# Halved weight loads and equal priority for both parts of h in the first stage of a hybrid decoder layer

## The chip, the core and the metric

The kernel runs on one core of a Trainium2 chip. The metric is the device time of one execution in microseconds; the time before is the median of three runs. The core has a matrix engine (TensorE, PE in the profile, with its weight loads as PEld), a vector engine (VectorE, DVE), an activation engine (ScalarE, ACT), a general engine (GpSimd, POOL), and SyncE (SP), whose queue issues nearly all DMAs here.

## The reference

One decoder layer on a sequence of 256 tokens with 2048 channels, all in float32. Cut to what matters:

```python
h = rms_norm(x, norm_w)                      # 256 x 2048
proj = h @ w_in                              # 2048 x 17440, split into the inputs of three branches
gates = sigmoid(g_logit + b_gate)            # one gate for each branch
y_a = pool_mixer(...)  @ w_br_pool           # causal pooling branch
y_b = ssd_mixer(...)   @ w_br_ssm            # chunked scan branch, gated with silu(z)
y_c = short_conv_mixer(...) @ w_br_conv      # gated short convolution branch
x = x + (gates[0]*y_a + gates[1]*y_b + gates[2]*y_c) @ w_out
return rms_norm(x, final_norm_w)
```

## The kernel before

Every float32 product is made of three matmuls on rounded parts: a number is split into a high part (rounded to the format fp32r) and the rest, and hi*hi, lo*hi and hi*lo are added up in PSUM. For weights `load_split` does this: SyncE loads a block into a buffer `raw` (line 122), ScalarE writes the high part `wh` (line 132), VectorE writes the rest `wl` (line 133). Lines 132 and 133 stand under `tc.high_priority(4000)`: the planner that puts the instructions of each engine in order takes them ahead of instructions that stand up to 4000 places earlier. `raw` has four buffers, `wh` and `wl` have three each. A buffer can be loaded again when all its readers are done.

The stage that the change touches is the first, "z01". It computes the first 832 columns of the projection (32 for dt, 800 for z) as two halves of 416 columns, before the RMS norm of x is known: it multiplies x times the norm's weight, and the norm's factor is applied afterwards. It walks over the 16 row tiles k of the projection (128 input channels each). For each k:

- `load_x` (line 216) loads two tiles of the transposed x at a time, for even k from 2 on.
- `make_h` (lines 201 to 212) makes the two parts of h: the high part on ScalarE (line 205; for k = 0 on VectorE, line 203), the rest on VectorE (line 206). It then squares x on ScalarE for the norm (line 208 for k = 0, line 211 for the others), and GpSimd adds the square to a sum (line 212). Nothing in `make_h` has a raised priority.
- `load_split` loads 128 x 832 weights (416 KB) with one DMA and splits them with one instruction on each of the two engines.
- twelve matmuls of 416 columns follow: for each half and each of the two token tiles hi*wh, lo*wh and hi*wl (lines 141, 142 and 143).

Tiles 0 and 1 of x and the first weights come in two special loads, r0 and r1, which are two of the four `raw` buffers. r0 holds the norm's weights, x of tile 0 and the left half of the weights of tile 0. r1 holds the right half of these weights and x of tile 1. So both are free only when the squares of tiles 0 and 1 have read them too. Below, w1, w2 and so on are the weight loads of tile 1, 2 and so on in the kernel before; the splits of tile 0 are already in halves.

Of the kernel before, what the change touches and what calls it, by code (L numbers as in the profile page):

```python
# [15 lines left out]
P = 128  # L16
D = 2048
SEQ = 256
KT = D // P
# [14 lines left out]
    + [("gate", 4 * b + n, [(O_GATE + 2048 * b + 512 * n, 512)]) for b in (2, 1) for n in range(4)]  # L34
)
XREST = 2
OUT_CHUNKS = (512, 512, 512, 256, 256)


# [24 lines left out]
def chunk_layout(k, widths):  # L64

    res, off = [], 0
    for n in widths:
        k0, ps = 0, []
        for kts in pieces(n, k):
            ps.append((off, k0, kts))  # L70
            off += P * kts * n
            k0 += kts
        res.append((n, ps))
    return res
# [9 lines left out]
def body(ctx, tc, x, xT, first, w_in, w_bp, w_bs, w_bc, w_o, pool_w, rows, smalls, consts, out):  # L84
# [16 lines left out]
    def s2t(name, bufs=2, dt=F32):  # L101
        return s2.tile([P, 512], dt, name=name, tag=name, bufs=bufs)

    def s1t(name, bufs=2):
        return s2.tile([P, SEQ], F32, name=name, tag=name, bufs=bufs)
# [9 lines left out]
    def rawt():  # L115
        return wp.tile([P, 1024], F32, name="raw", tag="raw", bufs=4)

    def load_split(src, off, kts, n, keep=False, raw=None):
        m = kts * n
        if raw is None:  # L120
            raw = rawt()
            dma(out=raw[:, :m], in_=src[off:off + P * m].rearrange("(p m) -> p m", p=P))
        pool, th, tl = (g4, "g4", "g4") if keep else (wp, "wh", "wl")
        wh = pool.tile([P, 1024], F32R, name="wh", tag=th)
        wl = pool.tile([P, 1024], F32R, name="wl", tag=tl)
        if n == 416:

            r, h, l = (w[:, :kts * q].rearrange("p (k n) -> p k n", k=kts)[:, :, :n] for w, q in ((raw, n), (wh, 512), (wl, 512)))
        else:
            r, h, l = (w[:, :m] for w in (raw, wh, wl))  # L130
        with tc.high_priority(4000):
            A.activation(h, r, AF.Copy)  # L132
            V.tensor_tensor(out=l, in0=r, in1=h.bitcast(F32), op=ALU.subtract)  # L133
        return [h, l] if n == 416 else [w.rearrange("p (k n) -> p k n", k=kts) for w in (h, l)]
# [4 lines left out]
    def mm3(acc, hi, lo, wh, wl, n, first, last):  # L139

        T.matmul(acc[:, :n], hi, wh, start=first, stop=False)  # L141
        T.matmul(acc[:, :n], lo, wh, start=False, stop=False)  # L142
        T.matmul(acc[:, :n], hi, wl, start=False, stop=last)  # L143
# [48 lines left out]
    xw = one.tile([P, KT * SEQ + 128], F32, name="xw", tag="yA")  # L192
# [4 lines left out]
    def xk(k):  # L197
        return xw[:, KT + k * SEQ:KT + (k + 1) * SEQ]

    def make_h(k, xr, nw, hi_on_v=False):  # L200
        h = h0[k // 2][:, k % 2]
        if hi_on_v:
            V.tensor_scalar(h[:, 0], xr, nw, None, op0=ALU.mult)
        else:
            A.activation(h[:, 0], xr, AF.Copy, scale=nw)  # L205
        V.scalar_tensor_tensor(out=h[:, 1], in0=xr, scalar=nw, in1=h[:, 0].bitcast(F32), op0=ALU.mult, op1=ALU.subtract)  # L206
        if k == 0:
            A.activation(sqs, xr, AF.Square)
        else:
            sq = s1t("cin")  # L210
            A.activation(sq, xr, AF.Square)
            G.tensor_tensor(out=sqs, in0=sqs, in1=sq, op=ALU.add)

    def load_x(k0, kts):
        a, b = KT + k0 * SEQ, KT + (k0 + kts) * SEQ
        dma(out=xw[:, a:b], in_=xT[:, a:b])
# [4 lines left out]
    def h0parts(k):  # L221
        return h0[k // 2][:, k % 2, 0], h0[k // 2][:, k % 2, 1]
# [10 lines left out]
    r0, r1 = rawt(), rawt()  # L233
# [3 lines left out]
    G.tensor_copy(xw[:, :KT], r0[:, :KT])  # L237
    for off, k, _ in where["z01", 0][1]:
        if k == 0:
            make_h(0, r0[:, KT:KT + SEQ], r0[:, :1], True)  # L240
            ws = [load_split(None, 0, 1, 416, raw=r) for r in (r0[:, KT + SEQ:], r1)]
            ws = [(wh[:, 0], wl[:, 0]) for wh, wl in ws]
        else:
            if k >= XREST and k % 2 == 0:
                load_x(k, 2)
            make_h(k, r1[:, 416:416 + SEQ] if k == 1 else xk(k), xw[:, k:k + 1])
            wh, wl = load_split(w_in, off, 2, 416)
            ws = [(wh[:, i], wl[:, i]) for i in range(2)]
        hi, lo = h0parts(k)
        for acc, (wh, wl) in zip(zacc, ws):  # L250
            for t in range(2):
                ts = slice(t * P, (t + 1) * P)
                mm3(acc[t], hi[:, ts], lo[:, ts], wh, wl, 416, k == 0, k == KT - 1)
    load_x(0, XREST)
    sm = one.tile([P, S_END], F32, name="sm")
# [236 lines left out]
    for g, w in enumerate(WIN):  # L492
# [6 lines left out]
        s, back, i = u0, 1, 1  # L499
        while back < w:  # L500
            nxt = win[i]
            V.tensor_tensor(out=nxt[:, :, PAD:], in0=s[:, :, PAD:], in1=s[:, :, PAD - back:PAD + SEQ - back], op=ALU.add)
            s, back, i = nxt, 2 * back, 3 - i
# [15 lines left out]
    for g in range(4):  # L519
        acc = in_channels("pg", g)  # L520
        yq = channels(pool_w, [(g * P * 512, 0, 2)], dhl[g], 2, [pss.tile([P, 512], F32, name="yq", tag="ss") for _ in range(2)])
        for b in range(2):
            k = 2 * g + b
# [34 lines left out]
    for j in range(4):  # L558
# [4 lines left out]
        for b, acc in enumerate(in_channels("cc", j)):  # L563
# [3 lines left out]
            k = 2 * j + b  # L567
# [40 lines left out]

    nch = len(OUT_CHUNKS)
    sso = one.tile([P, 2, nch], F32, name="sso")  # L610
# [32 lines left out]
    c0 = 0  # L643
    for i, (n, ps) in enumerate(chunk_layout(KT, OUT_CHUNKS)):
        fr = s2t("nw", bufs=2)
# [8 lines left out]
        else:  # L654
# [5 lines left out]
            ws = [load_split(w_o, off, kts, n, True) for off, _, kts in ps]  # L660
            for t in range(2):
                ts = slice(t * P, (t + 1) * P)
                for (wh, wl), (_, k0, kts) in zip(ws, ps):
                    for j in range(kts):
                        k = k0 + j
# [89 lines left out]
```

## Time and profile before

| | before |
|---|---|
| median of 3 runs | 1071.35 us (1070.44 to 1071.42) |
| profiled execution | 1071.29 us |
| its span, first to last instruction | 1069.2 us |
| PE busy | 1059.0 us (99%) |
| DVE busy | 715.5 us (67%) |
| ACT busy | 541.5 us (51%) |
| read from HBM | 208.57 MB, 197 GB/s over the span |

The profile is of one execution, whose span is 2.09 us shorter than its time. PE is busy nearly all the time, so the few places where it waits are what there is to look at; the views of these places are printed below, ahead of the prediction. Times in a row are microseconds from the start of the span unless marked ns.

### The profile page before, as it was taken

How to read it: one execution, taken by the hardware profiler on the slowest of the kernel's cores; microseconds unless marked ns; L12 is line 12 of the kernel's file. 1: busy time of each engine (PE TensorE's matmuls, PEld its weight loads, DVE VectorE, ACT ScalarE, POOL GpSimd, SP SyncE). 2: the span in 40 equal slices, each digit the busy share in tenths (PEclk: the TensorE clock that was granted, in tenths of full speed). 3: DMA queues.
4: the chain of work that ended last, by engine and by line, in shares of the span. 5: the costliest groups of instructions: out<-in, count | busy, mean ns of one | idle time of the engine just before them, and what ended most of it. 6: DMA issues, size and time to landing. Idle time of an engine off the chain costs nothing.

```text
span 1069.2 us, 14489 instructions
## 1 busy us (share of the span) xinstructions
PE 1059.0 (99%) x5486; PEld 917.1 (86%) x5486; DVE 715.5 (67%) x1011; ACT 541.5 (51%) x723; POOL 22.2 (2%) x35
## 2 busy tenths in 40 slices
PE   8999999999999999999999999999999999999997
PEld 7999888888888888888888888888888888888887
DVE  7596878777777666776875967565555555555564
ACT  7575666564465444554654645443444444444452
POOL 4100000000000000000000000000000000000000
PEclk9999999999999999999999999999999999999999
DMA  8766555555556566665556554555656666555663
GB/s 282 242 191 221 203 196 179 187 176 189 178 177 213 195 210 206 197 206 182 193 192 197 187 193 175 182 206 200 198 201 202 205 205 205 203 193 181 233 212 125
DMA packets 63141, 211.65 MB, mean 198 GB/s; under 512 B 6944, under 2 KB 7904, under 8 KB 63072
## 3 DMA queue, kind: packets, MB, share of 16 engines
q1 hardware_dynamic: 62784, 210.21, 58.6%
q8 instruction: 43, 0.70, 0.3%
q10 hardware_dynamic: 288, 0.52, 0.1%
q14 instruction: 26, 0.21, 0.1%
HBM read 208.57 MB, written 2.13 MB: 197 GB/s over the span
## 4 chain that ended last, share of the span: by engine, by line
PE 98%; issue 1%; DMA 0%; DVE 0%; ACT 0%; SPq 0%; POOLq 0%; POOL 0%; DVEq 0%
PE acc L169 25%; PE acc L142 19%; PE acc L143 19%; PE acc L141 19%; PE acc L173 13%; PE yp L457 1%; PE tp L410 1%; DMA raw<-w_in_c 0%; PE yq L169 0%; PE yo L463 0%; PE tpx L396 0%; PE yq L173 0%; PE cb L430 0%; DVE h L206 0%; ACT wh L132 0%
## 5 line engine op out<-in xcount | busy, mean ns | idle before, releaser
L133 DVE TENSOR_TENSOR wl<-raw,wh 128x1024 fp32r<-128x1024 f32 (+3 forms) x381 | 455.4, 1197 | 276.6 <-ACT wh L132 273.1
L132 ACT ACTIVATE wh<-raw 128x1024 fp32r<-128x1024 f32 (+3 forms) x381 | 394.3, 1036 | 382.8 <-PE acc L142 280.5
L169 PE MATMUL acc<-hl,wh 128*128 128x512 f32 x1152 | 280.0, 393 | 0.0
L169 PEld LDWEIGHTS acc<-hl,wh 128*128 128x128 f32 x1152 | 210.9, 188 | 41.4 <-issue 1.2
L173 PEld LDWEIGHTS acc<-hl,wl 128*128 128x128 f32 x1152 | 147.8, 191 | 5.6
L173 PE MATMUL acc<-hl,wl 128*128 128x256 f32 x1152 | 149.9, 283 | 0.0
L143 PE MATMUL acc<-wl,hl 128*128 128x512 f32 x384 | 149.4, 389 | 0.0
L142 PE MATMUL acc<-wh,hl 128*128 128x512 f32 x384 | 149.4, 389 | 0.0
L141 PE MATMUL acc<-wh,hl 128*128 128x512 f32 x384 | 149.4, 389 | 0.0
L142 PEld LDWEIGHTS acc<-wh,hl 128*128 128x128 f32 x384 | 72.1, 188 | 15.1
L141 PEld LDWEIGHTS acc<-wh,hl 128*128 128x128 f32 x384 | 72.1, 188 | 15.0
L143 PEld LDWEIGHTS acc<-wl,hl 128*128 128x128 f32 x384 | 72.1, 188 | 14.8
L185 ACT COPY half<-acc 128x256 f32<-128x256 f32 x72 | 26.3, 367 | 78.5 <-PE acc L169 78.5
L141 PE MATMUL acc<-wh,h 128*128 128x416 f32 x160 | 56.0, 353 | 1.2 <-ACT h L205 1.2
L142 PE MATMUL acc<-wh,h 128*128 128x416 f32 x160 | 56.3, 352 | 0.5 <-DVE h L206 0.5
L143 PE MATMUL acc<-wl,h 128*128 128x416 f32 x160 | 56.0, 351 | 0.0
L141 PE MATMUL acc<-wh,mT 128*128 128x512 f32 (+1 forms) x160 | 55.5, 348 | 0.0
L142 PE MATMUL acc<-wh,mT 128*128 128x512 f32 (+1 forms) x160 | 55.5, 347 | 0.0
L143 PE MATMUL acc<-wl,mT 128*128 128x512 f32 (+1 forms) x160 | 55.3, 347 | 0.0
L141 PE MATMUL acc<-wh,yh 128*128 128x512 f32 x128 | 50.0, 390 | 0.0
L143 PE MATMUL acc<-wl,yh 128*128 128x512 f32 x128 | 49.8, 389 | 0.0
L142 PE MATMUL acc<-wh,yl 128*128 128x512 f32 x128 | 49.8, 389 | 0.0
(183 smaller groups left out, 1035.0 us busy)
## 6 DMA issues: line engine op xcount, KB each, us to landing
raw<-w_in_c SPq DMA_DIRECT2D x240, 512.0 KB, 3.5
raw<-w_bs_c SPq DMA_DIRECT2D x32, 512.0 KB, 3.9
raw<-w_o_c SPq DMA_DIRECT2D x32, 512.0 KB, 4.1
raw<-w_in_c SPq DMA_DIRECT2D x39, 416.0 KB, 3.8
raw<-w_bp_c SPq DMA_DIRECT2D x16, 512.0 KB, 3.7
raw<-w_bc_c SPq DMA_DIRECT2D x16, 512.0 KB, 3.3
nw<-rows SPq DMA_DIRECT2D x19, 256.0 KB, 4.2
gm<-cumd SPq DMA_DIRECT2D x8, 512.0 KB, 5.0
```

The lines of the kernel that those rows point to most:

```text
L132: A.activation(h, r, AF.Copy)
L133: V.tensor_tensor(out=l, in0=r, in1=h.bitcast(F32), op=ALU.subtract)
L141: T.matmul(acc[:, :n], hi, wh, start=first, stop=False)
L142: T.matmul(acc[:, :n], lo, wh, start=False, stop=False)
L143: T.matmul(acc[:, :n], hi, wl, start=False, stop=last)
L169: T.matmul(acc[b], wh[:, j, b * P:(b + 1) * P], hl[:, k].rearrange("p i s -> p (i s)"), start=k == 0, stop=k == kt - 1)
L173: T.matmul(acc[b][:, SEQ:], wl[:, j, b * P:(b + 1) * P], hl[:, k, 0], start=False, stop=False)
L185: A.copy(half, acc[:, SEQ:])
L410: T.transpose(out=tp[:, b], in_=src[:, b * P:(b + 1) * P], identity=ident)
L457: T.matmul(yp[:, 64 * h:64 * h + 64], gm[:, h], xd[:, 64 * h:64 * h + 64], start=True, stop=True)
```

## The change

The weights of row tiles 1 to 3 are loaded in two DMAs of 208 KB (128 x 416) in place of one of 416 KB, and split by two instructions on each engine in place of one; the array in HBM is laid out to suit (for tile 0 the halves came in r0 and r1 already). Both parts of h are made under the same raised priority as the splits of weights. The squares leave `make_h`, keep their ordinary priority and now stand behind the load and the split of the tile's weights.

```diff
+HALVES = 4
...
         V.scalar_tensor_tensor(out=h[:, 1], in0=xr, scalar=nw, in1=h[:, 0].bitcast(F32), op0=ALU.mult, op1=ALU.subtract)
+
+    def square(k, xr):
         if k == 0:
             A.activation(sqs, xr, AF.Square)
...
     for off, k, _ in where["z01", 0][1]:
         if k == 0:
-            make_h(0, r0[:, KT:KT + SEQ], r0[:, :1], True)
+            with tc.high_priority(4000):
+                make_h(0, r0[:, KT:KT + SEQ], r0[:, :1], True)
             ws = [load_split(None, 0, 1, 416, raw=r) for r in (r0[:, KT + SEQ:], r1)]
             ws = [(wh[:, 0], wl[:, 0]) for wh, wl in ws]
         else:
             if k >= XREST and k % 2 == 0:
                 load_x(k, 2)
-            make_h(k, r1[:, 416:416 + SEQ] if k == 1 else xk(k), xw[:, k:k + 1])
-            wh, wl = load_split(w_in, off, 2, 416)
-            ws = [(wh[:, i], wl[:, i]) for i in range(2)]
+            with tc.high_priority(4000):
+                make_h(k, r1[:, 416:416 + SEQ] if k == 1 else xk(k), xw[:, k:k + 1])
+            if k < HALVES:
+                ws = [load_split(w_in, off + P * 416 * i, 1, 416) for i in range(2)]
+                ws = [(wh[:, 0], wl[:, 0]) for wh, wl in ws]
+            else:
+                wh, wl = load_split(w_in, off, 2, 416)
+                ws = [(wh[:, i], wl[:, i]) for i in range(2)]
+        square(k, r0[:, KT:KT + SEQ] if k == 0 else r1[:, 416:416 + SEQ] if k == 1 else xk(k))
...
         if s == "z01":
-            flat[:P * n * KT] = w.reshape(-1)
+            flat[:P * n * HALVES] = w[:HALVES].reshape(HALVES, P, 2, 416).transpose(0, 2, 1, 3).reshape(-1)
+            flat[P * n * HALVES:P * n * KT] = w[HALVES:].reshape(-1)
```

## Rows read from the trace of the kernel before

**Rows 1.** The page, part 4: chain that ended last, shares of the span by engine.

```profile
PE 98%; issue 1%; DMA 0%; DVE 0%; ACT 0%; SPq 0%; POOLq 0%; POOL 0%; DVEq 0%
```

**Rows 2.** Waits of PE, whole span: who waited for whom: total, times, longest.

```profile
PE acc L141 <- ACT h L205: 1.2, 1, 1.2
...
PE acc L142 <- DVE h L206: 0.5, 1, 0.5
```

**Rows 3.** Busy by stretch: from:to, length, engines' busy (instructions), granted clock, DMA, GB/s.

```profile
7.00:8.20 1.20, 0.08 (x1) 0.08 (x1) 0.50 (x1) 1.20 (x3) 0.00 (x0) 1.00 1.00 373
...
9.66:1052.00 1042.34, 1042.30 (x5386) 903.51 (x5387) 706.72 (x991) 533.71 (x711) 19.60 (x23) 1.00 0.59 199
```

**Rows 4.** Timeline, weight loads of PE: start, length, instruction, [idle before, releaser].

```profile
6.41 0.19 PEld L143 LDWEIGHTS acc<-wl,h 128*128 128x128 f32 x1
8.12 0.68 PEld L141 LDWEIGHTS acc<-wh,h 128*128 128x128 f32 x4 [1.52 <-ACT h L205]
9.66 0.19 PEld L142 LDWEIGHTS acc<-wh,h 128*128 128x128 f32 x1 [0.86 <-DVE h L206]
...
11.09 0.19 PEld L141 LDWEIGHTS acc<-wh,h 128*128 128x128 f32 x1
...
15.61 0.19 PEld L141 LDWEIGHTS acc<-wh,h 128*128 128x128 f32 x1
```

**Rows 5.** Timeline of ACT, from the second split to h of tile 1.

```profile
4.48 0.55 ACT L132 ACTIVATE wh<-raw 128x416 fp32r<-128x416 f32 x1 [0.28 <-DMA raw<-first]
4.94 0.40 ACT L208 ACTIVATE xc<-raw 128x256 f32<-128x256 f32 x1
6.77 0.90 ACT L132 ACTIVATE wh<-raw 128x832 fp32r<-128x832 f32 x1 [1.43 <-DMA raw<-w_in_c]
7.58 0.49 ACT L205 ACTIVATE h<-raw,xw 128x256 fp32r<-128x256 f32 x1
```

**Rows 6.** Timeline of DVE, from the splits of tile 0 to h of tile 1.

```profile
4.46 1.19 DVE L133 TENSOR_TENSOR wl<-raw,wh 128x416 fp32r<-128x416 f32 x2
7.70 1.02 DVE L133 TENSOR_TENSOR wl<-raw,wh 128x832 fp32r<-128x832 f32 x1 [2.05 <-ACT wh L132]
8.64 0.96 DVE L206 SCALAR_TENSOR_TENSOR h<-raw,xw,h 128x256 fp32r<-128x256 f32 x1
```

**Rows 7.** Timeline of SP's queue: issue of w1, w4, x of tiles 14 and 15, w13 and w14.

```profile
1.65 0.42 SPq L122 DMA_DIRECT2D raw<-w_in_c  x1
...
8.76 0.33 SPq L122 DMA_DIRECT2D raw<-w_in_c  x1
...
23.75 0.42 SPq L216 DMA_DIRECT2D xw<-x_chn  x1
26.07 1.26 SPq L122 DMA_DIRECT2D raw<-w_in_c  x2
```

**Rows 8.** Waits of SP's queue, first 12 us.

```profile
SPq L122 <- ACT xc L208: 0.3, 1, 0.3
```

**Rows 9.** Issue to landing: r0 and r1; w1; w4; x of tiles 2 and 3.

```profile
DMA to landing us min/median/max: 2.9/3.1/3.3
...
DMA to landing us min/median/max: 5.1/5.1/5.1
...
DMA to landing us min/median/max: 3.8/3.8/3.8
...
DMA to landing us min/median/max: 5.6/5.6/5.6
```

**Rows 10.** Groups by line and shape, first 40 us: count, busy us, mean ns, idle before.

```profile
L132 ACT ACTIVATE wh<-raw 128x832 fp32r<-128x832 f32 x16 | 14.2, 895 | 5.9 <-PE acc L142 4.1 <-DMA raw<-w_in_c 1.7
...
L133 DVE TENSOR_TENSOR wl<-raw,wh 128x416 fp32r<-128x416 f32 x2 | 1.2, 588 | 0.0
L132 ACT ACTIVATE wh<-raw 128x416 fp32r<-128x416 f32 x2 | 1.1, 551 | 1.9 <-DMA raw<-first 1.9
L206 DVE SCALAR_TENSOR_TENSOR h<-raw,h 128x256 fp32r<-128x256 f32 x1 | 0.5, 486 | 0.0
```

## The prediction, as it was put on record before the changed kernel ran

> **What bounds the kernel now.** The chain that ended last is PE for 98% [rows 1], so only what moves PE counts. The waits of PE are read next: over the whole span there are two on data, 1.2 us for the high part of h (ScalarE, line 205) and 0.5 us for its rest (VectorE, line 206) [rows 2]. The busy time by stretch confirms it from the other side: from 9.66 to 1052 us PE is busy 1042.30 of 1042.34 us [rows 3]. So all that the change can win lies before 9.66 us, in row tile 1, and what it wins reaches the end unless PE starts to wait somewhere else.
>
> How much is there? The timeline of PE's weight loads has the first load of tiles 2 and 4 at 11.09 and 15.61 [rows 4], so a tile takes PE 2.26 us, and tile 3 starts at 13.35. Tile 0 sends its last load at 6.41, so tile 1 could begin at 6.60 and tile 2 at 6.60 + 2.26 = 8.86. The most that can be won is 11.09 - 8.86 = 2.23 us, 0.21% of the time. The two idle stretches of the loads, 1.52 and 0.86 us [rows 4], are about this sum. 0.2% (2.14 us) is about what a measurement of this kernel can tell from no change.
>
> **Tile 1: h and halves.** ScalarE takes the second split of tile 0 (4.48 to 5.03), the square of tile 0 (to 5.34), then idles 1.43 us until w1 has landed, and makes h of tile 1 only after w1's split, at 7.58 [rows 5]. VectorE idles 2.05 us and makes the rest of h after the split of w1, at 8.64 [rows 6]. With raised priority the high part goes right behind the second split, 5.03 to 5.52 (0.49 [rows 5]); the rest goes behind VectorE's two half splits, which end at 5.65 [rows 6], and takes 0.49 [rows 10], to 6.14. Both are then done before PE wants them at 6.60. The weights: r1 landed at 4.48 [rows 5], and w1, issued at 1.65, 5.1 us later, at 6.75 [rows 7, 9]. The first half, 1a, is half of the bytes between, so about 5.6; the second, 1b, 6.75. A half split takes ScalarE 0.55 and VectorE 0.59 [rows 10]: 1a is split at 6.15 and 6.75, 1b at 7.3 and 7.9. PE wants 1a at 6.60 and 1b 1.13 later, at 7.73, and its first loads are those of the high parts. So tile 1 runs nearly without a wait, and 2.0 to 2.2 us are won at this point. This part I hold for safe.
>
> **What the halves add.** Per tile ScalarE gets 2 x 0.551 - 0.895 = 0.21 us more [rows 10], VectorE 2 x 0.588 - 1.02 = 0.16 [rows 6, 10], for three tiles 0.6 and 0.5. The idle 1.43 and 2.05 us of [rows 5, 6] hide them; without that cover each is paid once. SP gets three more issues of 0.33 to 0.42 us [rows 7], and x of tiles 2 and 3, issued right behind w1 and landed 5.6 us later [rows 9], at 7.7, comes one issue later, at 8.1 at worst. Its h is then made by 9.1, which is where tile 2 is wanted at best. The bytes stay the same. GpSimd's sums are not waited for by PE in this stage.
>
> **Tiles 2 to 4: the buffers.** Here the gain can go. There are four `raw` buffers and three of `wh`, and a half takes a whole one. Before, r0, r1, w1 and w2 filled the four; now r0, r1, 1a and 1b do, so nothing of tile 2 is on its way until a buffer is free. Which one is taken is seen on SP: w4 was issued at 8.76, when VectorE's split of w1 was done (7.70 + 1.02) [rows 6, 7], so the buffer that the planner sees free first is reused; w3 waited for the square of tile 0 [rows 8]. The first half of tile 2 (2a) thus goes out when the square of tile 0 has read r0 or when 1a is split on VectorE, at 6.75 plus the queue's step, 6.9. Were the square put right behind h of tile 1 it would be 5.9.
>
> No row has a half's flight alone. r0 (344 KB, an empty queue) took 2.9 [rows 9]; with 136 KB less at 373 GB/s [rows 3] that is 2.5, the lower bound. w4 (416 KB, shared queue) took 3.8 [rows 9]; with 208 KB less it is 3.2, the upper. I take 2.8. Then 2a lands at 9.7 and is split at 10.25 (ScalarE) and 10.85 (VectorE). Tile 2 begins at 10.25, not at 8.86: of the 2.2 us won 0.8 are left. The load of tile 4, whole again, is the ninth block, so it takes 2a's buffer at best (if every earlier one is free in its turn): issued 10.9, landed 3.8 later at 14.7, split on ScalarE 0.9 later at 15.6. PE began tile 4 at 15.61 before. Nothing is left in the middle of the bounds; with r0's buffer free a little earlier (a flight of 3.3, as r1 [rows 9]) it is 0.5. I take 0.3. Best ends: 2a issued 5.9, flight 2.5, w4's flight 3.3: split at 13.75, gain 1.9. Worst ends: 6.9, 3.2, and w4 4.4 (3.8 and the 0.6 of half a load ahead of it): 16.55, a loss of 0.9. That the low parts of w4 come 1.02 us behind [rows 6] costs nothing if PE is given the high parts of both halves first, as in [rows 4], where four loads of line 141 lead; else up to 0.7. From tile 5 on both the buffers and the loads are as before, and later weights stay ahead of PE [rows 3].
>
> The Trainium skill ("DMA: Bandwidth & Descriptors", Anatomy of one DMA) fits a DMA by about 2.0 us fixed plus its bytes at 436 GB/s, on another issue path than this one: a half gets barely cheaper than a whole. By it, as an estimate, a half flies 2.5 us and a whole 3.0, and tile 4 would be split 1.1 us sooner than in my sum. The trace agrees on the large fixed part for r0, and not on w4, which took 0.8 more [rows 9]; that is why I take the row.
>
> **The rivals.** *All of it is won.* 2a must land by 8.3, so be issued by 5.8 with a flight of 2.5; and w4 must be split by 13.4. Only the earliest place of the square and the lowest bounds come near: 1071.29 - 2.23 = 1069.05. Against it: four buffers.
>
> *Late squares starve the loads.* r0 and r1 come free only with the squares of tiles 0 and 1, and now all splits and all h go ahead of these on ScalarE. And h does not run dry: SP's queue lets x pass blocked weights (x of tiles 14 and 15 went out at 23.75, ahead of w13 and w14 at 26.07 [rows 7]), so h of later tiles is there to push the squares back. Behind ScalarE's queue then stand SP's loads for r0 and r1, and PE behind these. If the square of tile 0 comes only after the split of 3a, two buffers carry all: 2a split on VectorE at 10.85, 3a issued 10.9, landed 13.7, split 14.25: 0.9 later than tile 3 began before. The square then frees r0 at 14.65 (0.40 [rows 5]), w4 lands at 18.45, is split at 19.35, 3.7 us later than before: 1075.0. With the lower flights it is 2.5 us: 1073.8. It decides from where the square of tile 0 starts after 10.9; a square that only comes at 9 to 10 costs nothing. For it: the priorities; against it: ScalarE waits for data between 5 and 8 us [rows 5], where a square fits if the planner sees the gap.
>
> *The halves do nothing.* If 1a lands with 1b, or the planner's order stays, tile 1 is as before but for the extra work: 1071.3.
>
> A longer gap could cost PE its clock; through the 1.5 us gap of before the granted clock stayed at 1.00 [rows 3], so I leave that out.
>
> **How the numbers follow.** Forecast (the buffers eat nearly all): 1071.29 - 0.3 = 1071.0, its own range 1069.4 to 1072.2, chance 0.58. All won, 1069.05: 0.07. Starved by late squares, 1073.8 to 1075.0: 0.23. Nothing, 1071.3: 0.12. The median of the runs stands 0.06 above the profiled execution, which changes nothing. The range to hold 8 in 10 leaves out half of the first rival below and the dearer half of the second above: 1069.2 to 1074.4. Faster by over 0.2% (under 1069.2) is the first rival: 0.07. Slower (over 1073.5) is the second but for its cheapest cases: 0.21. The rest, 0.72, is within.
>
> **What would show it.** Step 1 is right if PE's waits on lines 205 and 206 are gone and tile 1's loads follow 6.60 with under 0.3 us idle. Step 2 is right if PE's new wait is on `wh` of the first half of tile 2 or on tile 4's, with SP waiting for `wl`. The starved case shows as a start of line 208 after 10 us and a wait of over 2 us on `wh` of tile 4. I would be wrong if tile 2 starts before 9.3 us, or if PE waits after tile 5.

## The result, and the profile after

| | before | after |
|---|---|---|
| median (6 runs each) | 1071.38 us (1070.44 to 1072.78) | 1077.1 us (1076.25 to 1077.44) |
| profiled execution | 1071.29 us | 1076.94 us |
| its span | 1069.2 us | 1074.8 us |

After over before is 1.0053, with a 95% interval of 1.0043 to 1.0063: the change costs 0.5%, some 5.7 us, and lies outside the predicted range. The two spans differ by 5.6 us, and that is what the traces have to account for. In the changed file the lines moved: the issue of a weight load is 123, the splits are 133 and 134, the matmuls 142 to 144, h is 206 and 207, and the squares are 211 (tile 0) and 214, with GpSimd's sum in 215.

The first view is again the timeline of PE's weight loads: start, length, instruction, and in brackets the idle time before it with its releaser. The lines are the first load of tiles 1 to 4, and between them the last two loads of tile 1 and one load from the middle of tile 3. They answer [rows 4].

```profile
7.39 0.19 PEld L142 LDWEIGHTS acc<-wh,h 128*128 128x128 f32 x1
...
9.27 0.19 PEld L143 LDWEIGHTS acc<-wh,h 128*128 128x128 f32 x1
9.46 0.19 PEld L144 LDWEIGHTS acc<-wl,h 128*128 128x128 f32 x1
11.62 0.19 PEld L142 LDWEIGHTS acc<-wh,h 128*128 128x128 f32 x1 [1.97 <-ACT wh L133]
...
16.36 0.29 PEld L142 LDWEIGHTS acc<-wh,h 128*128 128x128 f32 x1 [2.56 <-ACT wh L133]
...
18.26 0.33 PEld L142 LDWEIGHTS acc<-wh,h 128*128 128x128 f32 x1
...
21.21 0.19 PEld L142 LDWEIGHTS acc<-wh,h 128*128 128x128 f32 x1 [1.14 <-ACT wh L133]
```

Tile 1 runs without a wait. The waits that stood ahead of it and in its middle have gone to the tiles behind it: 1.97 us before tile 2, 2.56 before tile 3, 1.14 before tile 4, each for the high part of the weights. Twelve loads make a tile, so the same view dates every tile:

| first weight load of | before | after | later by |
|---|---|---|---|
| tile 1 | 8.12 | 7.39 | -0.73 |
| tile 2 | 11.09 | 11.62 | 0.53 |
| tile 3 | 13.35 | 16.36 | 3.01 |
| tile 4 | 15.61 | 21.21 | 5.60 |
| tile 9 | 26.91 | 32.61 | 5.70 |

The whole loss has been made by the start of tile 4. Of the step from tile 3 to tile 4 (4.85 us in place of 2.26), 1.14 us is the wait; the rest is tile 3 itself, whose loads take 0.33 us each and not 0.19. The busy time by stretch shows why: from:to, length, then busy time with instructions of PE, PEld, DVE, ACT and POOL, the granted clock, the DMA share and GB/s. The stretches are tile 2, the gap before tile 3, and most of tile 3.

```profile
11.60:13.80 2.20, 2.18 (x12) 2.17 (x12) 2.20 (x7) 2.20 (x6) 0.00 (x0) 1.00 0.85 289
13.80:16.30 2.50, 0.35 (x2) 0.00 (x1) 0.87 (x3) 2.09 (x8) 1.45 (x2) 1.00 0.85 248
16.36:19.60 3.24, 3.24 (x9) 3.14 (x10) 2.17 (x2) 1.95 (x5) 2.92 (x4) 0.50 0.90 309
```

After the gap the granted clock is 0.50, the lower of the two levels (1.2 GHz). Tile 3 takes 16.36 to 20.07, which is 3.71 us where a tile takes 2.26: 1.45 us of the loss.

Who was late? The next view is ScalarE's timeline, which answers [rows 5].

```profile
4.53 0.55 ACT L133 ACTIVATE wh<-raw 128x416 fp32r<-128x416 f32 x1 [0.42 <-DMA raw<-first]
4.99 0.49 ACT L206 ACTIVATE h<-raw,xw 128x256 fp32r<-128x256 f32 x1
5.62 1.21 ACT L133 ACTIVATE wh<-raw 128x416 fp32r<-128x416 f32 x2
7.42 3.71 ACT L206 ACTIVATE h<-xw 128x256 fp32r<-128x256 f32 x9 [0.58 <-DMA xw<-x_chn]
11.03 0.98 ACT L133 ACTIVATE wh<-raw 128x416 fp32r<-128x416 f32 x2
11.91 2.10 ACT L206 ACTIVATE h<-xw 128x256 fp32r<-128x256 f32 x5
13.91 0.40 ACT L211 ACTIVATE xc<-raw 128x256 f32<-128x256 f32 x1
14.22 0.40 ACT L214 ACTIVATE cin<-raw 128x256 f32<-128x256 f32 x1
...
15.46 0.42 ACT L214 ACTIVATE cin<-xw 128x256 f32<-128x256 f32 x1 [0.41 <-POOL xc L215]
15.78 0.97 ACT L133 ACTIVATE wh<-raw 128x416 fp32r<-128x416 f32 x2
...
19.96 0.42 ACT L214 ACTIVATE cin<-xw 128x256 f32<-128x256 f32 x1 [0.39 <-POOL xc L215]
20.28 0.88 ACT L133 ACTIVATE wh<-raw 128x832 fp32r<-128x832 f32 x1
```

The high part of h of tile 1 now stands right behind the second split, at 4.99. Then come fourteen more parts of h, nine and five in a row, with the two splits of tile 2 between them. Only at 13.91 does the square of tile 0 run, which ran at 4.94 before, and at 14.22 that of tile 1. Until then r0 and r1, two of the four buffers, are held. SP's queue shows the other end of this (it answers [rows 7, 8]): first its issues, then its waits in the first 20 us (who waited for whom: total, times, longest).

```profile
1.64 0.90 SPq L123 DMA_DIRECT2D raw<-w_in_c  x2
2.58 2.33 SPq L219 DMA_DIRECT2D xw<-x_chn  x5
6.82 0.99 SPq L123 DMA_DIRECT2D raw<-w_in_c  x2
7.87 1.37 SPq L219 DMA_DIRECT2D xw<-x_chn  x3
...
12.22 0.83 SPq L123 DMA_DIRECT2D raw<-w_in_c  x2
...
14.39 4.49 SPq L123 DMA_DIRECT2D raw<-w_in_c  x4
```

```profile
SPq L123 <- DVE wl L134: 5.9, 5, 2.2
SPq L123 <- DMA raw<-w_in_c: 1.6, 2, 0.9
SPq L123 <- ACT xc L211: 0.8, 1, 0.8
```

Weights go out in pairs: both halves of tile 1 (1a and 1b) at 1.64, of tile 2 (2a and 2b) at 6.82 (1a has been split), of tile 3 at 12.22 (2a has been split), and w4 at 14.39, when the square of tile 0 has freed r0. Between the pairs x passes: five loads, 1.3 MB, at 2.58 and three more at 7.87. So x of tiles 2 to 11 is there early, while weights are not, and the raised priority turns that x into h.

### The profile page after: what moved, and what is told of

The parts are those of the page before. It is cut to its first block, busy times and chain, and to the rows that moved or that the text cites. A ratio compares the mean times of both kernels' runs of the same rounds, so it can differ in the third digit from the quotient of the medians.

```text
span 1074.8 us, 14505 instructions
## 1 busy us (share of the span) xinstructions
PE 1061.8 (99%) x5486; PEld 919.0 (86%) x5486; DVE 712.8 (66%) x1014; ACT 542.6 (50%) x726; POOL 21.7 (2%) x35
## 4 chain that ended last, share of the span: by engine, by line
PE 97%; ACT 1%; issue 1%; DMA 0%; DVE 0%; SPq 0%; POOL 0%; POOLq 0%; DVEq 0%; ACTq 0%
PE acc L170 25%; PE acc L142 19%; PE acc L144 19%; PE acc L143 19%; PE acc L174 13%; PE yp L467 1%; PE tp L420 1%; ACT h L206 1%; DMA xw<-x_chn 0%; PE yq L170 0%; PE yo L473 0%; PE tpx L406 0%; ACT wh L133 0%; PE yq L174 0%; PE cb L440 0%
## 5 line engine op out<-in xcount | busy, mean ns | idle before, releaser
L142 PE MATMUL acc<-wh,h 128*128 128x416 f32 x160 | 58.1, 363 | 4.6 <-ACT wh L133 4.6
L143 PE MATMUL acc<-wh,h 128*128 128x416 f32 x160 | 57.1, 357 | 0.0
```

## The experiments

Each was timed beside the kernel before on the same chip, whose medians in these comparisons lie between 1071.26 and 1071.50 us. The medians are of eleven executions, of six for the changed kernel and e1, and of five for e16; a profile is of one of them. The edits are shown against the changed kernel. Four buffers for the halves (one half in each) and late squares are the two suspects, and the first kernels part them.

| kernel | median, us | ratio to before, 95% interval |
|---|---|---|
| changed kernel | 1077.1 | 1.0053 (1.0043 to 1.0063) |
| e1: halves alone | 1074.74 | 1.0033 (1.0020 to 1.0045) |
| e2: priority of h alone | 1073.06 | 1.0016 (1.0007 to 1.0025) |
| e3: changed kernel, squares raised too | 1072.58 | 1.0012 (1.0004 to 1.0021) |
| e4: changed kernel, squares off r0 and r1 | 1072.57 | 1.0012 (1.0003 to 1.0021) |
| e5: priority alone, squares raised too | 1070.48 | 0.9992 (0.9983 to 1.0001) |
| e9: only h of tile 1 raised, squares off r0 and r1, whole weights | 1070.31 | 0.9991 (0.9982 to 1.0000) |
| e12: halves alone, both in one buffer | 1071.62 | 1.0001 (0.9993 to 1.0010) |
| e14: e9 with tile 1 in halves, one buffer | 1070.53 | 0.9989 (0.9981 to 0.9998) |
| e15: changed kernel, halves in one buffer | 1072.94 | 1.0017 (1.0008 to 1.0025) |
| e13: e9 with tiles 1 to 3 in halves, one buffer | 1069.39 | 0.9983 (0.9974 to 0.9992) |
| e16: changed kernel, six buffers for squares | 1076.3 | 1.0048 (1.0034 to 1.0061) |
| e17: e15 with six buffers for squares | 1072.72 | 1.0013 (1.0004 to 1.0022) |

**Halves alone (e1).** h and the squares stand as in the kernel before, without a raised priority.

```diff
-            with tc.high_priority(4000):
-                make_h(k, r1[:, 416:416 + SEQ] if k == 1 else xk(k), xw[:, k:k + 1])
+            make_h(k, r1[:, 416:416 + SEQ] if k == 1 else xk(k), xw[:, k:k + 1])
+            square(k, r1[:, 416:416 + SEQ] if k == 1 else xk(k))
```

> Weights of tiles 1 to 3 in halves, but h and squares as in the kernel before (nothing raised, the square right behind h of its tile). Theory S (the squares, pushed behind all raised h, hold r0 and r1 and then stand in front of the weight splits on ScalarE): without the raise the square of tile 0 is early, at 6 to 8 us, and the loss is mostly gone: tile 4 begins at 15 to 17 us, 1070.5 to 1072.5. Rival B (eight half blocks in four raw buffers cost the time, whatever the priorities): tile 2 begins at 11 to 12, tile 4 at 19 to 21, 1074.5 to 1077.

It is 0.33% slower than before, so the halves cost by themselves; tile 4 begins at 18.51, between the two forecasts. The squares are not late here (5.98 and 8.24 us). PE waits before tile 1 for h, as in the kernel before, 0.81 us before tile 2 for weights, and longest before tile 4. Weight loads of PE, first load of that tile and two later ones, then SP's issues:

```profile
18.51 0.19 PEld L142 LDWEIGHTS acc<-wh,h 128*128 128x128 f32 x1 [2.36 <-ACT wh L133]
...
20.50 0.33 PEld L142 LDWEIGHTS acc<-wh,h 128*128 128x128 f32 x1
20.84 0.33 PEld L143 LDWEIGHTS acc<-wh,h 128*128 128x128 f32 x1
```

```profile
6.46 2.93 SPq L123 DMA_DIRECT2D raw<-w_in_c  x4
9.44 0.90 SPq L219 DMA_DIRECT2D xw<-x_chn  x2
12.43 2.93 SPq L123 DMA_DIRECT2D raw<-w_in_c  x4
```

w4, the ninth block, goes out only at 12.43 and lands 5.0 us later. Here too the clock falls behind the gap: from 19.6 to 23.0 us its mean is 0.51, and tiles 4 and 5 take 3.03 and 2.98 us in place of 2.26, 1.5 us together. This may not happen in every execution: three of the six have a mean granted clock of 0.997 over the span, the profiled one among them, and took 1075.0 to 1076.46 us; the three with 0.998 or 0.999 took 1074.13 to 1074.48. Without the fall the halves would then cost some 3.0 us.

**Halves alone, in one buffer (e12).** As e1, but the two halves of a tile lie in one buffer of `raw`, `wh` and `wl`; two DMAs and two splits on each engine remain.

```diff
+    def load_halves(off):
+        raw = rawt()
...
+        for i in range(2):
+            dma(out=raw[:, 416 * i:416 * (i + 1)], in_=w_in[off + P * 416 * i:off + P * 416 * (i + 1)].rearrange("(p m) -> p m", p=P))
...
-                ws = [load_split(w_in, off + P * 416 * i, 1, 416) for i in range(2)]
-                ws = [(wh[:, 0], wl[:, 0]) for wh, wl in ws]
+                ws = load_halves(off)
```

> Halves alone, as in the run with halves only, but both halves of a tile share one raw, one wh and one wl buffer, so the four raw buffers again hold four whole tiles; DMAs and splits are still of 416 columns. If the halves cost by taking up buffers: 1070.8 to 1071.8, as before. If they cost by their extra instructions or their smaller transfers: 1074 to 1075, as with halves only.

The loss of e1 is gone (1.0001), with the same number of loads and splits. What the halves cost is the buffers that they take, not their instructions. The edit gives back `raw`, `wh` and `wl` together; SP's waits point at `raw`, but no run parts the three.

**Priority alone (e2), and with early squares (e5).** Both load whole weights (`HALVES = 1`). e5 raises the squares as well:

```diff
+        with tc.high_priority(4000):
             square(k, r0[:, KT:KT + SEQ] if k == 0 else r1[:, 416:416 + SEQ] if k == 1 else xk(k))
```

> Both parts of h raised and squares behind the splits as in the change, but weights of tiles 1 to 3 whole. Theory S: r1 is held until the square of tile 1, and the squares still bunch up behind GpSimd's sums, so tile 4 begins at 17 to 20 us and the time is 1073 to 1076. Rival B: whole blocks keep two tiles in flight, tile 1 runs without a wait and nothing is lost later: 1069 to 1070.5.

> Whole weights, h and squares all raised. If the effects add up (halves +3.5 us, late squares +4, the raise of h in tile 1 -2.2, as the first four runs read), this is the raise alone: 1069.0 to 1070.0. If the raise of later h costs something by itself (h crowding the splits), 1071 or more.

e2 is 0.16% slower than before, e5 0.08% faster, with an interval that just takes in no change; the two intervals do not meet. e5 lies between its two forecasts. In e2 the time is in the range of the first theory, but tile 4 begins sooner than it said, at 16.51, and more is lost behind it (0.92 us of waiting for a low part in tile 5). ScalarE's timeline of e2:

```profile
9.37 0.40 ACT L211 ACTIVATE xc<-raw 128x256 f32<-128x256 f32 x1
9.67 0.89 ACT L133 ACTIVATE wh<-raw 128x832 fp32r<-128x832 f32 x1
10.46 2.49 ACT L206 ACTIVATE h<-xw 128x256 fp32r<-128x256 f32 x6
12.86 0.40 ACT L214 ACTIVATE cin<-raw 128x256 f32<-128x256 f32 x1
```

Six parts of h in a row push the square of tile 1 to 12.86, and r1 with it. So late squares cost by themselves too, 2.6 us from e5 to e2.

**The changed kernel with its squares out of the way (e3, e4).** e3 raises the squares as e5 does. e4 leaves the priorities and takes away the hold: the squares of tiles 0 and 1 read the copy of x that the kernel loads into `xw` behind this stage anyway, so r0 and r1 come free with their splits and h.

```diff
-        square(k, r0[:, KT:KT + SEQ] if k == 0 else r1[:, 416:416 + SEQ] if k == 1 else xk(k))
+        if k >= XREST:
+            square(k, xk(k))
...
+    for k in range(XREST):
+        square(k, xk(k))
```

> The changed kernel with the squares raised as well, so they stand in their place behind the splits of their tile. Theory S: r0 is read by 5.5 us and r1 by 7 us, no square waits in a bunch; tile 4 begins at 14.5 to 16.5 us: 1070.5 to 1072.5. Rival B: the halves are unchanged, so 1075 to 1077.

> The changed kernel (halves, all h raised, squares behind), but the squares of tiles 0 and 1 read the later copy of x, so r0 and r1 come free with the splits and h of tiles 0 and 1; the squares still come late and in bunches. If the late squares cost by holding r0 and r1: 3a and w4 are issued 4 to 5 us earlier and the time falls to 1072 to 1073.5. If they cost by standing in front of the splits on ScalarE, waiting for GpSimd: little is won, 1075 to 1077.

Either edit takes away 4.5 us of the 5.7 (e3 lies just above its range, and its tile 4 begins at 16.91). In e4 all parts of h are still raised and the first square runs at 11.65; only r0 and r1 are free. So the lateness costs by the buffers it holds. Of the loss that is left in e4, 0.5 us is there when tile 4 begins; a wait for a low part at 35.31, whose cause was not looked for, takes 0.7. SP's issues, ScalarE's split of w4, and PE's first load of tile 4 in e4:

```profile
5.15 3.62 SPq L123 DMA_DIRECT2D raw<-w_in_c  x4
8.83 0.90 SPq L219 DMA_DIRECT2D xw<-x_chn  x2
10.93 6.54 SPq L123 DMA_DIRECT2D raw<-w_in_c  x5
```

```profile
15.16 0.90 ACT L133 ACTIVATE wh<-raw 128x832 fp32r<-128x832 f32 x1 [0.38 <-DMA raw<-w_in_c]
```

```profile
16.11 0.19 PEld L142 LDWEIGHTS acc<-wh,h 128*128 128x128 f32 x1 [1.27 <-ACT wh L133]
```

**The changed kernel, halves in one buffer (e15).** The other way round: late squares stay, the buffers are given back.

> The changed kernel with one edit: the two halves of a tile still come by two DMAs and are split by two instructions, but share one buffer of raw, wh and wl. So 2a need not wait for a buffer, while the late squares still hold r0 and r1. Theory that the buffers of the halves and the late squares are two causes that add: the late squares of whole weights cost 2.6 us (1073.06 against 1070.48 with the squares off r0 and r1), one-buffer halves cost nothing, so 1072.5 to 1074, a wait of PE of 1.5 to 3 us before tile 3 and none before tile 2. Rival that the nine h in a row are the cause whatever the buffers: as the changed kernel, 1075.5 to 1077.5. Rival that the four buffers of the halves are needed for any loss: 1070.3 to 1071.5.

1072.94 is near e2 (1073.06), which has late squares and whole weights: the late squares still cost, and halves in one buffer add nothing to them. (The 1070.48 us that the expectation quotes is e5, where the squares are raised, not taken off r0 and r1.) PE has no wait before tile 2 (first load 9.01) and one of 1.24 us before tile 3, somewhat under what was expected there; the rest lies in waits for low parts and 0.63 us before tile 5.

**Squares that wait for GpSimd (e16, e17).** In the trace after, ScalarE stands behind squares that wait for a sum on GpSimd: 3.9 us in seven waits. The squares have two buffers. Here they rotate over six:

```diff
-            sq = s1t("cin")
+            sq = s1t(("cin", "ac", "sgc")[k % 3])
```

> The changed kernel with one edit: the squares rotate over six buffers in place of two, so that a square on ScalarE seldom waits for a sum on GpSimd. Theory that these waits, in front of splits on ScalarE, are a cause of their own: the split of 3a starts about 0.4 us sooner and that of w4 about 1.6 us sooner (it starts 1.6 us after its landing in the changed kernel), 1074.5 to 1076. Rival that they only fill time in which the splits could not be used: 1076.5 to 1077.5, tile 4 still begins near 21.

> The changed kernel with both halves of a tile in one buffer and with six buffers for the squares; r0 and r1 are still held by late squares. Theory that what is left in the version with one buffer and two buffers of squares (1072.94) is the hold of r0 and r1 alone: 1072.3 to 1073.3. Rival that a good part of it is ScalarE standing behind squares that wait for GpSimd: 1071 to 1072.

The waits for GpSimd are gone from ScalarE in e16, but the median falls by 0.8 us only, to a value between the two forecasts and with intervals that overlap. In the profiled execution the split of w4 now waits for its data:

```profile
19.22 0.40 ACT L214 ACTIVATE cin<-xw 128x256 f32<-128x256 f32 x1
21.80 0.90 ACT L133 ACTIVATE wh<-raw 128x832 fp32r<-128x832 f32 x1 [2.18 <-DMA raw<-w_in_c]
```

This trace is a poor measure of the edit: the execution was the longest of the five (1078.12 us), 1a landed 5.5 us after its issue and not 4.0 as in the changed kernel, which puts all that follows some 1.5 us later, and w4 flew 5.7 us and not 4.3. e17 does not differ from e15. The waits for GpSimd are thus no cause of their own that these runs can tell; whether they only lay over time in which the weights were not there yet is not shown.

**Versions that keep the gain (e9, e14, e13).** Only h of tile 1 is raised, and the squares read x as in e4. e9 has whole weights, e14 one halved tile and e13 three, both with one buffer for a tile.

```diff
-            with tc.high_priority(4000):
+            with tc.high_priority(4000 if k == 1 else 0):
```

> Whole weights; only h of tile 1 raised; the squares of tiles 0 and 1 read the copy of x that is loaded at the end of the stage anyway, so r0 and r1 never wait for a square (the sum starts with tile 2). Theory S: tile 1 loses its waits on h and only waits for its weights (6.8 us), r0 and r1 come free earlier than before: tile 2 begins at 9.8 to 10.3, 1.0 to 1.3 us are won, 1069.9 to 1070.4. Rival B says the same here. If it is not faster than before, something else bounds tiles 2 to 4.

> Only tile 1 in halves, both in one buffer; only h of tile 1 raised; squares of tiles 0 and 1 off r0 and r1. Tile 1 should run without a wait (as in the changed kernel) and tiles 2 to 4 as in the run with h of tile 1 raised alone: tile 2 begins at 9.0 to 9.6, 1.5 to 2.1 us are won over before: 1069.2 to 1069.9. If 1a lands no earlier than a whole w1 behind it, 1070.3 as in that run.

> Of the change: only h of tile 1 raised, the halves of tiles 1 to 3 in one buffer for each tile, the squares of tiles 0 and 1 read x from a second copy so that r0 and r1 come free with the splits. Theory: tiles 1 to 3 run without a wait (starts near 7.4, 9.7, 12.0), 1069.8 to 1070.8, as the same with one halved tile (1070.53). Rival that six more instructions on ScalarE and VectorE and three more issues cost something before tile 4: 1071 to 1072.

e9 came as expected. e14 was expected at 1069.2 to 1069.9 and is no better than e9: in its profile tile 1 runs without a wait, but tile 0 takes 0.8 us longer than in e13, and tile 2 waits 0.55 us for a low part. e13 is faster than expected and has the lowest median of all, 0.17% below the kernel before; its interval overlaps those of e5, e9 and e14, so a gain over them is not shown. In the profile of e13 tiles 1 to 4 start at 6.79, 9.05, 11.31 and 13.57, each 2.26 us behind the last: no wait at all, and 2.04 us sooner at tile 4 than before. From there on PE is as busy as before, 1042.30 of 1042.34 us:

```profile
9.66:1052.00 1042.34, 1042.30 (x5397) 903.48 (x5396) 706.09 (x992) 533.81 (x712) 19.60 (x24) 1.00 0.63 199
```

## Why the prediction failed

**What bounds the kernel: right.** All of the difference, after as before, lies in the first 22 us, and e13 shows that about 2 us was there to be won, as worked out.

**Step 1, tile 1: right.** h came at 4.99 to 5.48 (forecast 5.03 to 5.52) and tile 1 ran without a wait. The halves landed sooner than forecast: both were split on ScalarE by 6.83 (forecast 7.3). Tile 1 began at 7.39 and not at 6.60 because tile 0 itself ran 0.9 us longer (see what stays open).

**The halves' extra work costs nothing: right.** e12 has all of it and no loss.

**Step 2, the buffers: right in the first links, wrong in a flight.** 2a was issued at 6.82 (forecast 6.9), on the split of 1a, as the step says, and its sign came: PE waits for the high part of 2a, and SP for `wl`. The flight of 2a was 3.8 us, outside my ends of 2.5 and 3.2. The trace after shows both prices: 3a, issued at 12.22 into a queue with little else, flew 2.5 us, and 2a flew 3.8 behind x that SP had let pass. An estimate from the issues and the mean rate until then: 0.2 MB were still under way when 3a went out, and 1.0 MB when 2a did. I had made my upper end from w4 of the kernel before, and had not asked what else would be in the queue while the weights were blocked, although the prediction names x passing weights [rows 7].

By the estimate in the prediction, the Trainium skill ("DMA: Bandwidth & Descriptors", Anatomy of one DMA) gives a half 2.5 us. The trace agrees for 3a and not for 2a.

In e4, where r0 and r1 are free, the rest of the step can be read: w4 was issued at 10.93 (forecast 10.9), flew 4.1 us (forecast 3.8), and tile 4 began at 16.11 (forecast 15.6). That the issue agrees is luck: 2a went out at 5.15, into r0's buffer and 1.75 us sooner than forecast, and flew 4.3 us, 1.5 longer. With 1072.57 us e4 stands just above the forecast's own range (to 1072.2), so without the late squares the forecast would have been missed by little. In e1, with unraised h, the same chain runs later, issue 12.43 and flight 5.0, and there the clock adds 1.5 us.

**The step that failed: w4 goes out at 10.9 "if every earlier one is free in its turn".** r0 and r1 were not, and w4 went out at 14.39. The rival "Late squares starve the loads", taken for unlikely (0.23) and priced too low, is what happened. The point named for it was a square of tile 0 after 10.9; it came at 13.91. The argument against it was that ScalarE waits for data between 5 and 8 us, where a square fits. ScalarE did wait, 0.58 us before 7.42, and the square did not run, though its x had landed by 3.6: in the order of the engine, which the planner had made, fifteen parts of h stood ahead of it. The fact that sets their number is in [rows 7], and I used it for one sentence.

Its price was 2.5 to 3.7 us (by its own flights the lower end is 2.6), and it was 5.6. Followed along w4, from the forecast's chain to the trace:

| | forecast | after | difference |
|---|---|---|---|
| w4 issued | 10.9 | 14.39 | 3.5 |
| its flight | 3.8 | 4.3 | 0.5 |
| landed to start of the split | 0 | 1.6 | 1.6 |
| split on ScalarE | 0.9 | 0.9 | 0 |

That is 5.6 us from 15.6 to 21.2. The rival's own chain had w4 issued at 14.65 and landed at 18.45, and the trace has 14.39 and 18.7. The path is right, the times are in part luck: the rival put the square of tile 0 behind the split of 3a and 3a's issue at 10.9, and the trace has the square ahead of that split (13.91 and 15.78) and the issue at 12.22. What it lacked is the 1.6 us between landing and split, in which ScalarE stood behind squares. But e16 takes GpSimd's waits out of ScalarE and its median is no more than 0.8 us lower, so this term is how the trace adds up, and it is not shown that removing it alone gives it back.

Seen from PE instead, 1.45 us of the loss is tile 3 at half clock, **the term that the prediction left out** on the ground that a gap of 1.5 us had left the clock at 1.00. It priced the rival at up to 3.7 us of waiting and did not ask what such a gap does. The two readings are of one loss, and are not to be added. The split of w4 writes the third `wh` buffer back, that of 2b, which PE had left with tile 2, so it did not wait for tile 3: at full clock PE would only have stood longer before tile 4. The other way round, a split of w4 right at its landing (18.7) would have been done by 19.6, but tile 3 sent its last load only at 19.88, so tile 4 would have begun about 1.1 us sooner than 21.21 and not 1.6. This is worked out and not shown; the 0.8 us of e16 does not speak against it. What the clock costs by itself in the changed kernel is open; in e1, where nothing waited behind it, it is 1.5 us.

**Do the two causes add?** Four kernels, all with every h raised, differ in these two things alone: e5 has neither, e3 the halves in four buffers, e2 the late squares, and the changed kernel both. From e5 it is 2.1 us to e3, 2.6 to e2 and 6.6 to the changed kernel, 1.9 more than the sum of 4.7. Each ratio is known to about 0.1%, or 1 us, so the 1.9 is about as large as its own error. It is also near the 1.45 us that tile 3 lost at half clock: in the profiles of e2, e3 and e5 the granted clock stays at 1.00 through the first 26 us. That both causes together made gaps that brought the clock down, where neither did alone, fits these rows and is not shown by itself; in e1, with unraised h, the halves alone were enough.

**What stays open.** In the profile after, the first six weight loads of tile 0 take 0.29 to 0.34 us, before 0.19, though the granted clock reads 1.00; tile 0 is 0.9 us longer by it. The profiles of e1, e2, e4, e5, e12, e14 and e17 have it too, and those of the kernel before, e3, e9, e13, e15 and e16 do not (at most in the first load); so it follows none of the edits, and neither its cause nor its share in the medians is known. Nor was it tried to keep x from passing the weights on SP's queue by itself.

## What to carry to other kernels

A raised priority is paid for by whatever reads the same buffers at the old one: before raising a step, list who else holds its inputs, and how many raised steps can be ready before that reader has its turn. A load cut in two wants one buffer for both parts, or it halves the depth of prefetch. While blocked loads wait, ask what is put ahead of them in the queue: 2a flew 3.8 us in place of 2.5 with that traffic under way.

## What was not expected of the hardware

PE's clock fell to half behind gaps such as these: 2.56 us without a weight load before tile 3 of the changed kernel (granted clock 0.50 from 16.36 to 19.60) and 2.36 us before tile 4 of e1. It stayed at 1.00 behind 1.97 us before tile 2 of the changed kernel. The length of a gap does not settle it: in e16 the clock stayed at 1.00 through tile 2, behind 2.40 us, and fell in tile 3, behind 2.36. The first load of each of these tiles, and one more of each:

```profile
12.56 0.19 PEld L142 LDWEIGHTS acc<-wh,h 128*128 128x128 f32 x1 [2.40 <-ACT wh L133]
12.86 0.19 PEld L142 LDWEIGHTS acc<-wh,h 128*128 128x128 f32 x1
...
17.34 0.19 PEld L142 LDWEIGHTS acc<-wh,h 128*128 128x128 f32 x1 [2.36 <-ACT wh L133]
...
18.71 0.33 PEld L142 LDWEIGHTS acc<-wh,h 128*128 128x128 f32 x1
```

In e1 the first six loads behind the gap still took 0.19 us, at 1.00, and only then did the clock fall:

```profile
18.50:19.50 1.00, 0.99 (x5) 0.99 (x6) 1.00 (x1) 1.00 (x3) 0.59 (x1) 1.00 0.94 373
19.60:23.00 3.40, 3.40 (x12) 3.24 (x11) 3.40 (x4) 3.08 (x7) 1.31 (x2) 0.51 0.72 187
```

The flight of 2a or 3a (208 KB) was 2.5 us in a queue with little in it, and 3.8 behind five loads of x; in e4 it was 4.3 behind three of them, so the number of loads ahead does not set it. The flight of w4 (416 KB) was 4.3 us in the changed kernel, 4.1 in e4, 5.0 in e1 and 5.7 in the profiled execution of e16.
